# A transformer layer in split fp32: where the remainder of the down projection's weights is computed

## The chip, the cores and the metric

The kernel runs on one NeuronCore of one Trainium2 chip. The metric is device time in microseconds of one execution; lower is better. Before the change the median of 3 runs is 771.91 us (771.39 to 772.88).

## The reference

One layer of a diffusion backbone over 512 latent tokens and 128 context tokens, all in float32, with a model width of 1024 and an inner width of the feed-forward part of 2816. Each kind of token has its own modulation (scale, shift and gate made from a condition vector):

```python
mod = (jax.nn.silu(cond) @ w_ada + b_ada)[:, None, :]
sh1, sc1, g1, sh2, sc2, g2 = jnp.split(mod, 6, axis=-1)
h = _rms(x, norm_mix) * (1 + sc1) + sh1
mix, k, v = _mixer(h, rope, ctx_k, ctx_v, w_in, q_norm, k_norm, conv_w,
                   attn_out_norm, conv_out_norm, w_out)
x = x + g1 * mix
h2 = _rms(x, norm_ffn) * (1 + sc2) + sh2
gate, up = jnp.split(h2 @ w_gate_up, 2, axis=-1)
x = x + g2 * ((jax.nn.silu(gate) * up) @ w_down)
```

The mixer is grouped-query attention beside a short gated convolution. The change touches the last line alone: the product with `w_down`, a matrix of 2816 by 1024.

## The kernel before

All 640 tokens are worked on as five tiles of 128 (four latent, one context). The matrix products run on TensorE (PE) in fp32r, a rounded form of float32. To keep float32's accuracy each operand is split in a rounded part (hi) and the remainder (lo = operand − hi), and each product is made of three: hi·hi, lo·hi, hi·lo (`mm3`, lines 154 to 157). `split` (lines 150 to 152) makes the two parts: ScalarE (ACT) writes the rounded part (line 151), VectorE (DVE) subtracts it from the operand (line 152).

The weights arrive as a stream of blocks, planned in the order of their use. `load` (line 218) takes a buffer `wf` (three of them), issues the load from HBM on SP's queue (line 225), and calls `load_split` (line 237), which takes a buffer `wh` and a buffer `wl` (four of each) and splits the block into them. `W` (line 256) hands a block to its product and, before that, loads the blocks that come up to 3 places later (9 for gate and up blocks). The blocks of the first norm's output weights (`gain`) are scaled while they are split; all others take the plain path, line 244.

The feed-forward part works in four groups of 6, 6, 5 and 5 feature tiles of 128. In a group, gate and up products of each feature tile come first, in Winograd's form: seven products of 12 matmuls each, with operands that are quarters of the loaded blocks or sums of quarters (`op_load`, line 195). These operands are split too, into buffers of the same `wh` and `wl` rings, in turn. DVE makes the sums (line 207). Products leave PSUM by ACT's copies (`copy_of`, line 1125) and DVE's sums (lines 1138, 1154, 1157, 1164); the activations end as the split pair `gH`, `gL`.

Then the group's down projection runs (`down`): two halves of 512 output columns, and in each half blocks of two feature tiles (128 partitions by 2 × 512 values, 512 KB; in the groups of five the last block of a half holds one tile, 256 KB). There are 24 such blocks in all. The first block of a half is used up for all five token tiles; the second and third are used in turn, token tile by token tile. Each sum is multiplied by `g2` (line 1230) and added to `x2` (line 1231); in the last group the outputs are stored from there.

PE's instructions keep the order of the program. For the other engines a planner orders the instructions by priorities and its own estimate of their times; within an engine they then run in that order, and an instruction that waits holds up those behind it. `early(n)` moves instructions up by n places of priority; for the plain split n is `SOW` = −300, that is, back. A buffer of a ring is written again only when all readers of its last content are done.

POOL (GpSimd) makes some powers, sums and sums of quarters for the first four feature tiles (`SPO` = 4), and issues a few small loads near the start. DMA transfers are issued from SP's queue nearly always.

Of the kernel before, what the change touches and what calls it, by code (L numbers as in the profile page):

```python
# [15 lines left out]
P = 128  # L16
# [63 lines left out]
SOW = -300  # L80
# [11 lines left out]
def build(ctx, tc, x_prompt, x_sample, c, cache_k, cache_v, c_ctx, norm_mix, norm_ffn, w_ada, b_ada,  # L92
# [66 lines left out]
    def rstd_of(ss, n, scale, extra=None, tag="rs"):  # L159
        """(ss * scale + eps) ** -0.5 (times extra)"""  # L160
        w = ss.shape[1]
        ms = T("ms", (P, w), F32, 4)
        dve.tensor_scalar(ms, ss, scale, EPS, ALU.mult, ALU.add)
        r = T(tag, (P, w), F32, 6)
        pool.tensor_tensor(r, ms, neghalf[:, :w], ALU.pow)
        if extra is not None:
            dve.tensor_scalar_mul(r, r, extra)
        return r
# [7 lines left out]

# [1 line left out]
    x_dram = [x_sample[0, t * P:(t + 1) * P, :] for t in range(NL)] + [x_prompt[0]]  # L178
# [6 lines left out]

# [1 line left out]
    order, place, stream_at, phase = [], {}, [0], [0]  # L187
# [7 lines left out]
    def op_load(e):  # L195
        """one stationary operand of a gate and up block: a quarter of the block, or a sum of quarters"""
        f, name = e[0][1:]
        g, u = (order[place[x, f]][5] for x in "gu")
        a11, a12, a21, a22 = g[:, 0:4], g[:, 4:8], u[:, 0:4], u[:, 4:8]
        if name[0] == "S":  # L200
            if name == "S1":
                sums[f] = T("sx", (P, 2, 4, P), F32, 2)
            s13, s24 = sums[f][:, 0], sums[f][:, 1]
            src, x, y, op = {"S1": (s13, a21, a22, ALU.add), "S2": (s24, s13, a11, ALU.subtract),
                             "S3": (s13, a11, a21, ALU.subtract), "S4": (s24, a12, s24, ALU.subtract)}[name]
            with early(SOP[f >= NPLAIN]):
                (pool if f < SPO else dve).tensor_tensor(src, x, y, op)
        else:
            src = {"A11": a11, "A12": a12, "A21": a21, "A22": a22}[name]
        w = T(("wh", "wl")[ops[0] % 2], (P, 2, 4, P), F32R, WHB)  # L210
        ops[0] += 1
        with early(SOP[f >= NPLAIN]):
            split(w[:, 0], w[:, 1], src)
        e[5] = w
# [22 lines left out]
    def load_split(e, wf):  # L237
        key, src, ph, ring, gain, _ = e
        a, b = src.shape[1], src.shape[2]
        wh = T(ring + "h", (P, a, b), F32R, WHB)  # L240
        wl = T(ring + "l", (P, a, b), F32R, WHB)
        if gain is None:
            with early(SOQ[key[1]] if key[0] == 'q' else SOW):
                split(wh, wl, wf)
        else:
            for i in range(a):
                g = vec[:, gain + i:gain + i + 1]
                act.activation(wh[:, i], wf[:, i], AF.Copy, scale=g)
                dve.scalar_tensor_tensor(wl[:, i], wf[:, i], g, f32(wh[:, i]), ALU.mult, ALU.subtract)
        e[5] = (wh, wl)  # L250
# [61 lines left out]

# [1 line left out]
    crow = T("crow", (16, P))  # L314
# [3 lines left out]
    def ada1_load(k):  # L318
        """w_ada of feature tile k of the first norm's scale and shift"""
        out = []  # L320
        for h in range(2):
            wf = T("af", (P, 4, 2, P), F32, AFB)
            for i, col in enumerate((D + k * P, k * P)):
                sp.dma_start(wf[:, :, i], wa[:, 4 * h:4 * h + 4, col:col + P])
            out.append(wf)
            yield
        ada1[k] = out
        yield
# [41 lines left out]
    dve.tensor_copy(cs, cps.rearrange("p (c k) -> p k c", c=2))  # L370
    # products with the two conditions: four contraction tiles at a time on the four column groups of the
    # array, each with its conditions in the first columns; the groups' sums are added by sel afterwards
    dve.tensor_copy(cp[:, :, 0:2], cs)
# [11 lines left out]
    def vec_do():  # L385
        vps = PB((P, 64))
        pe.transpose(vps, rows, ident[:64, :64])
        dve.tensor_copy(vec[:, 0:64], vps)
        # (1 + b_sc) * norm for both norms
        for i, (bo, no) in enumerate(((8, V_MIX), (32, V_FFN))):  # L390
            dve.scalar_tensor_tensor(nb[:, i], vec[:, bo:bo + KD], 1.0, vec[:, no:no + KD], ALU.add, ALU.mult)

# [1 line left out]
    modA = [T(f"modA{i}", (P, KD, 2)) for i in range(2)]  # L394
    modB = [T(f"modB{i}", (P, KD, 2)) for i in range(2)]

    def mod_evict(i, f0, n, ps_sc, ps_sh):
        """ps_*: [P, n, 2] sums without bias for features f0..f0+n tiles"""
        no = (V_MIX, V_FFN)[i]
        bo = (0, 24)[i]  # L400
        if ps_sc is not None:
            tmp = T("modt", (P, n, 2), F32, 2)
            dve.tensor_tensor(tmp, ps_sc, vec[:, no + f0:no + f0 + n].unsqueeze(2).to_broadcast([P, n, 2]), ALU.mult)
            dve.tensor_tensor(modA[i][:, f0:f0 + n, :], tmp,
                              nb[:, i, f0:f0 + n].unsqueeze(2).to_broadcast([P, n, 2]), ALU.add)
        if ps_sh is not None:
            dve.tensor_tensor(modB[i][:, f0:f0 + n, :], ps_sh,
                              vec[:, bo + f0:bo + f0 + n].unsqueeze(2).to_broadcast([P, n, 2]), ALU.add)

# [1 line left out]
    hH = [T(f"hH{k}", (P, TOK), F32R) for k in range(KD)]  # L411
# [22 lines left out]
    def xT_do(t):  # L434
        """the normed tokens of tile t, feature-major"""
        both = PS2() if t < XB else None
# [121 lines left out]

# [1 line left out]
    rt = T("pr", (P, 2, NL, HD), F32, PRB)  # L560
# [19 lines left out]
    def head_norm(ps, nh, t, which):  # L580
        """rms over each head, gain, rotary; ps [P, nh*64] -> SBUF f32 [P, nh, 64]"""
        w = nh * HD
# [23 lines left out]

# [1 line left out]
    KA = T("KA", (P, NKV, 768), F32R)  # L608
# [52 lines left out]

# [1 line left out]
    g1 = [T("g1", (P, D), F32, 2) for _ in range(2)]  # L663
# [3 lines left out]
    CH = [(0, 320), (320, 320)]  # L667
    # (chunk, columns of the chunk, token columns, columns of the padded row)
    PIECES = [(0, slice(0, 320), slice(0, 320), slice(1, 321)),
# [106 lines left out]

# [1 line left out]
    of = [None] * NT  # L778
# [66 lines left out]
    def att_add(t, v, e):  # L845
        # the rows of the v lo products go to the other half of the partitions
        esw = T("es", (P, 2, P))
# [11 lines left out]

    # the context tokens' queries: four heads at a time  # L860
    cu = {}
# [45 lines left out]

# [1 line left out]
    units = [unit(t, v, p) for t in range(NL) for v in range(NKV) for p in range(2)]  # L909
# [35 lines left out]

# [1 line left out]
    if DSI:  # L947
# [32 lines left out]
    def g2_step(j, kp):  # L980
        """a quarter of g2's columns: sums over the contraction on the vector engine, then over partitions"""
        w = W(("ada", 5, j, kp))
# [18 lines left out]

    # second operands of the gate and up products: quarters of h2 (contraction half, token half) and their sums
    B = {}
# [79 lines left out]

    # ---- SwiGLU: a gate block and its up block by half the contraction against half the tokens, seven products
    # for the eight (Winograd's form) ----
    close_pool("psum")
# [15 lines left out]
    def plain(f, bs, toks):  # L1102
        """gate and up blocks of one half of the tokens by plain products"""
        ps = [FB(), FB()]
        for x, a in zip(ps, ("A1", "A2")):
            for i in (1, 2):
                prod(x, f, f"{a}{i}", bs[i - 1], i == 1, i == 2)
        if toks is LO:
            st[f] = T("cg", (P, TOK), F32, 2), T("cu", (P, TOK), F32, 2)
        cg, cu = st[f]  # L1110
        act.activation(cg[:, toks], ps[0][:, :HALF], AF.Silu)
        dve.tensor_tensor(cu[:, toks], ps[1][:, :HALF], cg[:, toks], ALU.mult)
        if toks is HI:
            ff_out(f, cu)
            del st[f]
# [161 lines left out]
def _rope_constants():  # L1277
    """cos and signed sin of the axial angles, [512 tokens, 64]: they depend on the shapes alone"""
    import numpy as np
# [36 lines left out]
```

## Time and profile before

| | before |
|---|---|
| runs, median (lowest to highest) | 771.91 us (771.39 to 772.88) |
| profiled execution, span from first to last instruction | 771.6 us |
| mean granted TensorE clock | 0.989 |
| bytes moved by DMA | 84.53 MB, mean 110 GB/s |
| down blocks loaded | 20 of 512 KB, 4 of 256 KB |
| down projection, four groups: PE from | 414.4, 532.4, 636.0, 732.6 us |
| last matmul ends | 767.7 us |

For the profiled execution the span is the only time that is given; it lies 0.3 us under the median of the runs. Busy times are per engine; PE is TensorE's matmuls, PEld its weight loads, which overlap them. A row of a timeline gives start, duration, engine, line, operation, the tile written and the tiles read; what stands in square brackets is idle time ahead of it and what ended that.

### The profile page before, as it was taken

Reading aid. Unit: us, or ns where it says so; the run is one execution under the profiler, and the core shown is the slowest. Engines: PE = TensorE matmul, PEld = TensorE weight load, DVE = VectorE, ACT = ScalarE, POOL = GpSimd, SP = SyncE. Lnnn points to the kernel's source line nnn. Section 1 sums busy time; section 2 is a strip of 40 time slices with the busy share of each in tenths; the row PEclk is TensorE's granted clock in tenths of the full one; section 3 lists DMA queues with packets and bytes.
Section 4 is the critical chain, followed back from the end, with each engine's and each line's share of the span. In section 5 each row is a group of like instructions: output and inputs, shape, how many; then the busy total and the mean of one; then the engine's idle time right before and its main releaser. Section 6 shows DMA issues by size and latency. Waiting matters only on the chain.

```text
span 771.6 us, 11961 instructions
## 1 busy us (share of the span) xinstructions
PE 744.2 (96%) x4580; PEld 669.2 (87%) x4580; DVE 563.1 (73%) x1033; ACT 376.8 (49%) x732; POOL 70.8 (9%) x97
## 2 busy tenths in 40 slices
PE   4999999999999999996999999999999999999997
PEld 3778988989999787886998789999889998899986
DVE  5566887675666799789778777984677866788653
ACT  5446676666665346875452125554125542255510
POOL 3105101011010330044100000000000000000000
PEclk9999999999999999999899999999999999999999
DMA  9984134424325433111134412233112231222312
GB/s 290 308 236 128 42 109 140 121 90 140 120 89 171 161 133 110 56 55 55 56 110 153 134 55 83 83 109 110 54 56 82 83 109 56 80 84 84 110 55 82
DMA packets 102350, 84.53 MB, mean 110 GB/s; under 512 B 4526, under 2 KB 82674, under 8 KB 102292
## 3 DMA queue, kind: packets, MB, share of 16 engines
q1 hardware_dynamic: 100980, 83.39, 35.0%
q8 instruction: 36, 0.59, 0.3%
q10 hardware_dynamic: 1056, 0.26, 0.2%
q0 software_dynamic: 256, 0.11, 0.1%
q14 instruction: 22, 0.18, 0.1%
HBM read 79.68 MB, written 2.75 MB: 107 GB/s over the span
## 4 chain that ended last, share of the span: by engine, by line
PE 83%; DVE 8%; ACT 3%; DMA 2%; issue 2%; SPq 2%; POOL 1%; ACTq 0%; POOLq 0%
PE pf L155 17%; PE pf L157 17%; PE pf L156 17%; PE pc L678 3%; PE pc L679 3%; PE pc L680 3%; PE ps L155 3%; PE ps L156 3%; PE ps L157 3%; PE po L833 2%; PE ps L790 2%; PE pt L816 2%; PE pc L380 2%; DMA af<-in_w_ada_dram 2%; DVE wl L152 1%
## 5 line engine op out<-in xcount | busy, mean ns | idle before, releaser
L151 ACT ACTIVATE wh<-wf 128x1024 fp32r<-128x1024 f32 (+1 forms) x76 | 64.1, 843 | 93.1 <-PE pf L157 63.2
L155 PE MATMUL pf<-wh,gH 128*128 128x512 f32 (+1 forms) x225 | 88.2, 392 | 0.0
L157 PE MATMUL pf<-wh,gL 128*128 128x512 f32 (+1 forms) x225 | 87.7, 390 | 0.0
L156 PE MATMUL pf<-wl,gH 128*128 128x512 f32 (+1 forms) x225 | 87.7, 390 | 0.0
L152 DVE TENSOR_TENSOR wl<-wf,wh 128x1024 fp32r<-128x1024 f32 (+1 forms) x42 | 49.4, 1176 | 27.8 <-ACT wh L151 24.9
L678 PE MATMUL pc<-hH,wh 128*128 128x320 f32 x192 | 61.7, 321 | 0.0
L679 PE MATMUL pc<-hL,wh 128*128 128x320 f32 x192 | 60.0, 312 | 0.0
L680 PE MATMUL pc<-hH,wl 128*128 128x320 f32 x192 | 59.9, 312 | 0.0
L155 PE MATMUL pf<-T,wh 128*128 128x320 f32 x160 | 50.1, 313 | 6.2 <-ACT p L1125 6.2
L155 PEld LDWEIGHTS pf<-wh,gH 128*128 128x128 f32 x225 | 42.3, 188 | 9.8 <-ACT wh L151 0.2
L157 PEld LDWEIGHTS pf<-wh,gL 128*128 128x128 f32 x225 | 42.3, 188 | 9.8
L156 PEld LDWEIGHTS pf<-wl,gH 128*128 128x128 f32 x225 | 42.3, 188 | 9.8 <-issue 0.2
L156 PE MATMUL pf<-T,wh 128*128 128x320 f32 x160 | 49.9, 312 | 0.0
L157 PE MATMUL pf<-T,wh 128*128 128x320 f32 x160 | 49.9, 312 | 0.0
L155 PE MATMUL pf<-T,wl 128*128 128x320 f32 x160 | 49.3, 308 | 0.0
L156 PE MATMUL pf<-T,wl 128*128 128x320 f32 x160 | 49.3, 308 | 0.0
L157 PE MATMUL pf<-T,wl 128*128 128x320 f32 x160 | 49.3, 308 | 0.0
L156 PE MATMUL pf<-B,wl 128*128 128x320 f32 x152 | 47.5, 313 | 0.3 <-DVE B L1020 0.3
L155 PE MATMUL pf<-B,wl 128*128 128x320 f32 x152 | 47.4, 312 | 0.0
L157 PE MATMUL pf<-B,wl 128*128 128x320 f32 x152 | 47.2, 310 | 0.0
L1230 DVE TENSOR_TENSOR dm<-pf,g 128x512 f32<-128x512 f32 (+1 forms) x41 | 27.7, 676 | 22.9 <-PE pf L157 22.9
L151 ACT ACTIVATE wl<-wf 128x512 fp32r<-128x512 f32 x34 | 21.4, 630 | 43.5 <-PE pf L156 36.8
(308 smaller groups left out, 2097.5 us busy)
## 6 DMA issues: line engine op xcount, KB each, us to landing
wf<-in_w_gate_up_dram SPq DMA_DIRECT2D x44, 512.0 KB, 3.8
aw<-in_w_ada_dram SPq DMA_DIRECT2D x24, 512.0 KB, 4.7
wf<-in_w_down_dram SPq DMA_DIRECT2D x20, 512.0 KB, 3.2
wf<-in_w_in_dram SPq DMA_DIRECT2D x18, 512.0 KB, 5.9
af<-in_w_ada_dram SPq DMA_DIRECT2D x32, 256.0 KB, 6.1
x<-in_x_sample_dram SPq DMA_DIRECT2D x8, 512.0 KB, 5.3
wf<-in_w_out_dram SPq DMA_DIRECT2D x8, 512.0 KB, 4.5
wf<-in_w_ada_dram SPq DMA_DIRECT2D x8, 512.0 KB, 3.8
```

What stands on the lines that cost most here:

```text
L151: act.activation(hi, src, AF.Copy)
L152: dve.tensor_tensor(lo, src, f32(hi), ALU.subtract)
L155: pe.matmul(out, lh, rh, start=start, stop=False, skip_group_check=more)
L156: pe.matmul(out, lh, rl, start=False, stop=False, skip_group_check=more)
L157: pe.matmul(out, ll, rh, start=False, stop=stop, skip_group_check=more)
L380: pe.matmul(out[CG * g:CG * (g + 1)], cp[:, k], w, start=(k < 4), stop=(k >= KD - 4), skip_group_check=True)
L678: pe.matmul(acc, wh[:, k], hH[k][:, c0:c0 + n], start=(k == 0), stop=False)
L679: pe.matmul(acc, wh[:, k], hL[k][:, c0:c0 + n], start=False, stop=False)
L680: pe.matmul(acc, wl[:, k], hH[k][:, c0:c0 + n], start=False, stop=(k == KD - 1))
L790: pe.matmul(s2[:, g, :320], q, kk[:, v, P + g * 320:P + (g + 1) * 320], start=(i == 0), stop=(i == 1))
L816: pe.transpose(tp[:, i, h], u[3][h][:, kt * P:(kt + 1) * P], ident)
L1230: dve.tensor_tensor(dm, ps[:, :n], g2[cc][:, oc], ALU.mult)
```

## The change

For a block of `w_down`, `split` is no longer called. ACT writes the rounded part into `wh` as before, and then, in a second pass over `wf`, the same with a scale of −1 into `wl`: the negated rounded part. POOL then issues a transfer that reads the same block once more from HBM and adds it onto `wl`. What stands in `wl` after it is block − rounded part, as before. All three carry the same low priority as the split had. The comments and descriptions that the diff also takes out are left out here.

```diff
         wh = T(ring + "h", (P, a, b), F32R, WHB)
         wl = T(ring + "l", (P, a, b), F32R, WHB)
-        if gain is None:
+        if key[0] == "d":
+
+            with early(SOW):
+                act.activation(wh, wf, AF.Copy)
+                act.activation(wl, wf, AF.Copy, scale=-1.0)
+                pool.dma_start(wl, src, accum_op=ALU.add)
+        elif gain is None:
             with early(SOQ[key[1]] if key[0] == 'q' else SOW):
                 split(wh, wl, wf)
         else:
```

## The prediction

> **What bounds the kernel now.** I read the page first, for the engines' shares, then the busy time by stages from the first down block on, then what the weight loads of TensorE (PEld) waited for, and last the timelines of ACT, DVE and PE around the 24 down blocks.
>
> ```profile
> PE 744.2 (96%) x4580; PEld 669.2 (87%) x4580; DVE 563.1 (73%) x1033; ACT 376.8 (49%) x732; POOL 70.8 (9%) x97
> ```
>
> ```profile
> core 0: us, PE busy (x) PEld busy (x) DVE busy (x) ACT busy (x) POOL busy (x), PEclk, DMA share, GB/s
> 402.00:768.00 366.00, 365.65 (x2109) 334.91 (x2108) 265.13 (x422) 137.09 (x240) 0.00 (x0) 1.00 0.28 87
> 414.00:437.00 23.00, 23.00 (x100) 18.07 (x98) 19.99 (x30) 5.54 (x7) 0.00 (x0) 1.00 0.51 160
> 460.00:530.00 70.00, 70.00 (x479) 70.00 (x478) 56.43 (x94) 38.63 (x71) 0.00 (x0) 1.00 0.31 96
> ```
>
> ```profile
> PEld pf L155 <- ACT p L1125: 6.4, 1, 6.4
> PEld pf L155 <- DVE cu L1154: 0.3, 1, 0.3
> ```
>
> The reader is to see three things. PE is busy for 365.65 of the 366 us in which every down block is rounded and used, at a granted clock of 1.00. DVE is busy for 265 of them and nothing on PE waits for it: the only wait of note after 366 us, 6.4 us, is for an ACT copy in a stage before the first down block is touched. And POOL does nothing at all in that time. So an instruction taken off DVE here can give at most 366.00 − 365.65 = 0.35 us. The change can only keep the time or cost something.
>
> **What is removed.** The 24 subtractions on DVE:
>
> ```profile
> L152 DVE TENSOR_TENSOR wl<-wf,wh x24: 685/1222/1226, 404.2 to 750.3; 128x1024 fp32r<-128x1024 f32 x20, 128x512 fp32r<-128x512 f32 x4
> ```
>
> 20 × 1.22 + 4 × 0.69 = 27.2 us of DVE, all under a busy PE: worth 0 to 0.35 us; I take 0.
>
> **What is added.** On ACT a second pass over each block (the negated rounded part), of the form of the one that is there:
>
> ```profile
> 552.24 1.06 ACT L151 ACTIVATE wh<-wf 128x1024 fp32r<-128x1024 f32 x1 [11.54 <-PE pf L157]
> 749.64 0.63 ACT L151 ACTIVATE wh<-wf 128x512 fp32r<-128x512 f32 x1 [8.74 <-PE pf L157]
> ```
>
> 20 × 1.06 + 4 × 0.63 = 23.7 us of ACT, which now is busy for 137 of the 366 us. Then one transfer from POOL's queue for each block. No row shows an accumulating transfer, so I bound it from its neighbours: plain loads of the same blocks from SP, and POOL's few small loads.
>
> ```profile
> wf<-in_w_down_dram SPq DMA_DIRECT2D x20, 512.0 KB, 3.2
> wf<-in_w_down_dram SPq DMA_DIRECT2D x4, 256.0 KB, 2.6
> gnq<-in_q_norm_dram POOLq DMA_DIRECT2D x1, 32.0 KB, 5.8
> gnk<-in_k_norm_dram POOLq DMA_DIRECT2D x1, 32.0 KB, 5.0
> ```
>
> ```profile
> 18.50 0.96 POOL L508 DMA_DIRECT2D gnq<-in_q_norm_dram  x1
> 19.45 0.56 POOL L508 DMA_DIRECT2D gnk<-in_k_norm_dram  x1
> 369.24 1.27 POOL L207 TENSOR_TENSOR sx<-wf,sx 128x512 f32<-128x512 f32 x1
> ```
>
> From SP, 256 KB more cost 3.2 − 2.6 = 0.6 us, so 512 KB move in about 1.2 us and 2.0 are fixed. An accumulating transfer also reads its destination: 1.2 more. POOL's issue takes 0.56 to 0.96. Lower bound 3.2 (as the plain load), upper bound 5.8 (POOL's slowest small landing, when the loads at the start crowd the queues) + 1.2 + 1.2 = 8.2. I take 3.2 + 1.2 + 0.96 = 5.4 us from issue to landing, an estimate, because the transfers of this stage meet a DMA share of 0.28, like the SP rows, while POOL's small rows come from the crowded start. The last work of POOL is the row at 369.24, so the 24 issues have nothing queued behind them, and SP's queue is not moved past anything. The transfers read 20 × 512 + 4 × 256 KB = 11 MB more, in 366 us about 30 GB/s on top of 87.
>
> The Trainium skill, DMA: Bandwidth & Descriptors, section "Anatomy of one DMA", gives a transfer issued from GpSimd about 2.0 us plus its bytes over 436 GB/s; for 512 KB that would be an estimate of 3.2 us, the same as the SP row here, and less than the POOL rows of 5.0 and 5.8 us show for 32 KB. By it the transfer would be hidden with more to spare; the page gives no time for an accumulating one.
>
> **Whether it is hidden.** wl of a block comes later than now, by the difference of (ACT pass + transfer) and (subtraction): 1.06 + 5.4 − 1.22 = 5.2 us. What hides it is the time between the rounding of a block and its first use, which PE fills with earlier products. The tightest two that I found:
>
> ```profile
> 553.33 1.23 DVE L152 TENSOR_TENSOR wl<-wf,wh 128x1024 fp32r<-128x1024 f32 x1 [1.12 <-ACT wh L151]
> 561.79 0.40 PE L155 MATMUL pf<-wh,gH 128*128 128x512 f32 x1
> 562.02 0.39 PE L156 MATMUL pf<-wl,gH 128*128 128x512 f32 x1
> ```
>
> ```profile
> 626.38 1.05 ACT L151 ACTIVATE wh<-wf 128x1024 fp32r<-128x1024 f32 x1
> 627.47 1.23 DVE L152 TENSOR_TENSOR wl<-wf,wh 128x1024 fp32r<-128x1024 f32 x1 [0.45 <-ACT wh L151]
> 636.22 0.40 PE L156 MATMUL pf<-wl,gH 128*128 128x512 f32 x1
> ```
>
> The first is the third block of a half (its buffer comes free at 552.24, when the second block of the half before is used up), the second the first block of a group. With both ACT passes back to back, 2.12 us, the transfer may take 562.02 − 552.24 − 2.12 = 7.7 us in the one and 636.22 − 626.38 − 2.12 = 7.7 us in the other. 5.4 fits with 2.3 to spare; 8.2 would miss by 0.5. The first block of all has more:
>
> ```profile
> 402.37 1.06 ACT L151 ACTIVATE wh<-wf 128x1024 fp32r<-128x1024 f32 x1 [1.12 <-PE pf L157]
> 405.89 1.06 ACT L151 ACTIVATE wh<-wf 128x1024 fp32r<-128x1024 f32 x1 [0.69 <-ACT gH L151]
> 407.66 1.23 DVE L152 TENSOR_TENSOR wl<-wf,wh 128x1024 fp32r<-128x1024 f32 x1 [1.47 <-ACT wh L151]
> 414.68 0.40 PE L156 MATMUL pf<-wl,gH 128*128 128x512 f32 x1
> ```
>
> 414.68 − 402.37 − 2.12 = 10.2 us, less a wait for the wl buffer. That wait is the new one on ACT: the subtraction at 407.66 began 0.7 us after its wh was done (405.89 + 1.06 = 406.95), so its buffer was freed by PE then, and 1.77 us after the wh buffer. ACT will stand there in order in DVE's place, up to 1.77 − 1.06 = 0.7 us, and behind it stand ACT's copies of product sums, for which DVE's sums and then PE wait:
>
> ```profile
> 411.18 0.44 ACT L1125 ACTIVATE u<-pf 128x320 f32<-128x320 f32 x1 [0.82 <-PE pf L157]
> 411.74 0.48 DVE L1154 TENSOR_TENSOR cu<-pf,u 128x320 f32<-128x320 f32 x1
> 412.69 0.31 PE L155 MATMUL pf<-B,wl 128*128 128x320 f32 x1
> ```
>
> This chain ends at 411.74 + 0.48 = 412.22 and PE needs it at 412.69: 0.47 us of slack. An ACT pass of 1.06 us just ahead of such a copy would cost PE 1.06 − 0.47 = 0.6 us. SOW = −300 sets the passes behind the copies in the planner's eyes, and ACT is busy for only 38.63 of the 70 us in that stage, so I take one such hit, 0.6 us, lower bound 0. The load buffer wf is now released after the second ACT pass in place of the subtraction: 2.12 against 1.06 + 1.22 us after the start of the rounding, no worse; if it came 1 us later, the next load from SP would, and only DVE's sums of quarters wait for those.
>
> **The sum.** Against the profiled execution, whose span is 771.6 us: −0 (DVE) + 0 (transfer hidden) + 0.6 (one copy delayed) = 772.2 us. The runs shown have a median of 771.91, 0.3 above that span and no more than their own spread; I leave the forecast at 772.2, no change that a measurement of this kernel can tell (about 0.2%, 1.5 us).
>
> **The rivals.**
> Late remainder (slower): the accumulating transfer takes more than 7.7 us from issue to landing, and PE stands at the first use of wl. The mechanism has one place, the weight load of line 156 in the down projection, and decides from 7.7 us on. For it: POOL's only rows are 5.0 and 5.8 us for a sixteenth of the bytes, and the read of the destination may be slower than a plain move. Against: the crowd at the start. Price: at 10 us the two tight blocks cost 2.3 each, and the others, whose slack runs from 9 us (four or so, as the first block after its buffer wait), about 0.6 each: 4.6 + 2.4 = 7.0, giving 779. At 12 us, 2 × 4.3 + 4 × 2.5 = 18.6, giving 790.
> The Trainium skill, SBUF — State Buffer, section "Who interferes with whom", speaks against the change: GpSimd, which writes the descriptors of such a transfer, shares ports with VectorE and stands still while a two-port VectorE instruction holds them, though tensor_tensor, nearly all of what DVE does here, is inferred not to block it. If every busy us of DVE blocked POOL (265 of 366), the issue would stretch from 0.96 to 0.96 / 0.28 = 3.4 us and the transfer to 7.9: an estimate just over the edge. No run here shows it yet.
> ACT in the way (slower): about half of the 24 passes fall into gate and up stages, and half of those are placed ahead of a copy: 6 × 0.6 = 3.6, plus waits of 0.7 for a buffer in two: 5.0, giving 776.6. For it: the slack of 0.47. Against: ACT's idle time and the priority.
> A gain (faster): the other instructions are placed anew around the shorter DVE queue and the 6.4 us wait at 366 us shrinks, say by half: 768.4. For it: nothing but that the planner sees a changed program. Against: the wait lies before the first down block.
> That the change does not do what it says would be a transfer that lands in no more time than the subtraction took: then all is as in the forecast.
>
> **How the numbers follow.** Hidden, 0.46 (772.2; its own range 771.0 to 773.4, all within 0.2% of 771.9); late remainder 0.35; ACT in the way 0.15; gain 0.04. Hence slower 0.50, same 0.46, faster 0.04. The range runs from 770.9, the whole of the 0.35 us and the runs' spread below the median, up to 784, where the late remainder is cut at about 11 us of transfer; the gain and the upper third of the late case, together 0.15, are left out.
>
> **What would show it.** Right: 24 rows of POOL issues of 0.6 to 1 us, landing in 4 to 7 us; ACT about 24 us busier, DVE 27 less; PE still without a gap from 402 to 768 us. Wrong: PEld waits at line 156 for a DMA of w_down into wl (late remainder), or PE waits at line 155 for ACT copies at line 1125's place in the new file or DVE sums behind them (ACT in the way).

## The result, and the profile after

The changed kernel takes 779.52 us (median of 4 runs, 776.72 to 782.83) against 771.67 before: a ratio of 1.0098, 95% interval 1.0073 to 1.0123. It is slower by about 1%. Its profiled execution is the fastest of the four, 776.72 us, with a span of 775.0; all later runs show the same 1.7 to 2.3 us around the span.

The page of the changed kernel, the lines that answer to those of before and to the prediction's terms (busy us and share; a queue's packets, MB and share; a group's busy us and mean ns, then idle time and its releaser; KB and median us to landing):

```profile
PE 744.1 (96%) x4580; PEld 667.3 (86%) x4580; DVE 538.2 (69%) x1009; ACT 397.5 (51%) x756; POOL 99.3 (13%) x121
...
q0 software_dynamic: 6272, 11.65, 8.6%
...
L247 POOL DMA_DIRECT2D wl<-in_w_down_dram x24 | 27.8, 1158 | 357.5 <-ACT wl L246 348.3
...
L246 ACT ACTIVATE wl<-wf 128x1024 fp32r<-128x1024 f32 (+1 forms) x24 | 23.6, 984 | 47.9 <-PE pf L156 44.2
...
wf<-in_w_down_dram SPq DMA_DIRECT2D x20, 512.0 KB, 3.6
wl<-in_w_down_dram POOLq DMA_DIRECT2D x20, 512.0 KB, 8.3
```

The 24 issues are there (27.8 us of POOL), ACT has its second pass (23.6 us), DVE is 563.1 − 538.2 = 24.9 us less busy. None of that moves PE's busy time. The number that stands out is 8.3 us to landing, where a plain load of the same block from SP has 3.6. What PE waited for, in the same kernel from 366 us on:

```profile
PE pf L156 <- DMA wl<-in_w_down_dram: 4.2, 1, 4.2
```

One wait, once, in the whole down projection. The timeline around it, rows of SP, ACT, POOL and PE in order of time:

```profile
405.66 0.37 SPq L225 DMA_DIRECT2D wf<-in_w_down_dram  x1
...
405.94 1.22 POOL L247 DMA_DIRECT2D wl<-in_w_down_dram  x1 [1.61 <-PE pf L157]
...
412.61 1.06 ACT L245 ACTIVATE wh<-wf 128x1024 fp32r<-128x1024 f32 x1 [4.41 <-DMA wf<-in_w_down_dram]
413.58 1.04 ACT L246 ACTIVATE wl<-wf 128x1024 fp32r<-128x1024 f32 x1
...
414.92 1.22 POOL L247 DMA_DIRECT2D wl<-in_w_down_dram  x1 [7.76 <-ACT wl L246]
...
419.43 0.40 PE L155 MATMUL pf<-wh,gH 128*128 128x512 f32 x1
424.08 0.79 PE L156 MATMUL pf<-wl,gH 128*128 128x512 f32 x1 [4.25 <-DMA wl<-in_w_down_dram]
```

The same load in the kernel before, its issue on SP and the ACT pass that waited for it:

```profile
408.91 0.37 SPq L225 DMA_DIRECT2D wf<-in_w_down_dram  x1
...
412.24 1.06 ACT L151 ACTIVATE wh<-wf 128x1024 fp32r<-128x1024 f32 x1 [0.62 <-DMA wf<-in_w_down_dram]
```

This is the third block of the first half of the first group. Two delays add up. Its plain load, issued on SP at 405.66, now ends the wait of ACT at 412.61: 6.9 us, where before it took 412.24 − 408.91 = 3.3. Beside it run the accumulating transfers of the two blocks ahead, issued at 403.04 and 405.94, which take 7.2 and 10.3 us to landing. Then its own transfer, issued at 414.92, releases PE at 424.08, 9.2 us later. Stages of the changed kernel around the stall (start and end, length, busy us and count of PE, PEld, DVE, ACT, POOL, granted clock, DMA share, GB/s):

```profile
411.00:419.80 8.80, 8.80 (x39) 6.76 (x37) 4.61 (x8) 3.11 (x4) 1.22 (x1) 1.00 0.87 186
419.80:424.10 4.30, 0.05 (x2) 0.03 (x1) 1.75 (x3) 0.00 (x0) 0.00 (x0) 0.76 0.90 277
424.10:428.00 3.90, 3.90 (x9) 3.11 (x10) 3.65 (x6) 2.00 (x2) 0.18 (x1) 0.50 0.34 105
428.00:432.00 4.00, 4.00 (x17) 3.16 (x16) 2.52 (x4) 2.01 (x2) 1.53 (x2) 0.90 0.78 224
...
436.00:440.00 4.00, 4.00 (x17) 2.73 (x16) 0.00 (x0) 2.52 (x3) 1.20 (x1) 1.00 1.12 231
```

The DMA engines are nearly full here: 0.87 and 0.90 of their time, later 1.12 (in this view the share can pass 1), and 0.85 from 411 to 440 us as a whole; before, the first down stage had 0.51. And the stall costs more than its length: when PE starts again, its granted clock is 0.50, and only later 1.00. From the first matmul of the first half to that of the second are 440.02 − 411.03 = 29.0 us, against 436.76 − 414.44 = 22.3 before: 6.7 us lost, of them 4.25 of standing still and 2.4 at the lower clock. The half speed lasts from 422.0 to 428.8; finer stretches show its two ends (0.67 over half a microsecond is one third of it at full speed):

```profile
421.50:422.00 0.50, 0.00 (x0) 0.00 (x0) 0.05 (x1) 0.00 (x0) 0.00 (x0) 1.00 1.04 324
422.00:422.50 0.50, 0.00 (x0) 0.00 (x0) 0.00 (x0) 0.00 (x0) 0.00 (x0) 0.50 1.01 332
...
428.50:429.00 0.50, 0.50 (x3) 0.43 (x2) 0.50 (x1) 0.00 (x0) 0.50 (x1) 0.67 0.36 41
429.00:429.50 0.50, 0.50 (x4) 0.41 (x3) 0.17 (x1) 0.32 (x1) 0.02 (x1) 1.00 0.71 164
```

PE works at half speed from 424.08 to 428.8, 4.7 us, and half of that is the 2.4. The other groups lost nothing that counts: from first to last matmul their down projections take 42.0, 35.0 and 35.2 us, against 42.0, 35.0 and 35.1 before.

### The profile page after: what moved, and what is told of

Same layout as the page of the kernel before. It is cut to its first block, busy times and chain, and to the rows that moved or that the text cites. A ratio compares the mean times of both kernels' runs of the same rounds, so it can differ in the third digit from the quotient of the medians.

```text
span 775.0 us, 12020 instructions
## 1 busy us (share of the span) xinstructions
PE 744.1 (96%) x4580; PEld 667.3 (86%) x4580; DVE 538.2 (69%) x1009; ACT 397.5 (51%) x756; POOL 99.3 (13%) x121
## 3 DMA queue, kind: packets, MB, share of 16 engines
q0 software_dynamic: 6272, 11.65, 8.6%
## 4 chain that ended last, share of the span: by engine, by line
PE 80%; DVE 8%; DMA 3%; ACT 3%; issue 3%; SPq 1%; POOL 1%; DVEq 0%; POOLq 0%; ACTq 0%
PE pf L156 17%; PE pf L155 17%; PE pf L157 17%; PE pc L684 3%; PE pc L685 3%; PE pc L686 3%; PE ps L155 3%; PE ps L156 3%; PE ps L157 3%; PE po L839 2%; PE ps L796 2%; PE pt L822 2%; PE pc L386 2%; DMA af<-in_w_ada_dram 2%; DMA wl<-in_w_down_dram 1%
## 5 line engine op out<-in xcount | busy, mean ns | idle before, releaser
L247 POOL DMA_DIRECT2D wl<-in_w_down_dram x24 | 27.8, 1158 | 357.5 <-ACT wl L246 348.3
L151 ACT ACTIVATE wh<-wf 128x512 fp32r<-128x512 f32 (+1 forms) x52 | 40.4, 777 | 25.5 <-DMA wf<-in_w_in_dram 8.1
L246 ACT ACTIVATE wl<-wf 128x1024 fp32r<-128x1024 f32 (+1 forms) x24 | 23.6, 984 | 47.9 <-PE pf L156 44.2
```

The source lines that it names most:

```text
L151: act.activation(hi, src, AF.Copy)
L246: act.activation(wl, wf, AF.Copy, scale=-1.0)
L247: pool.dma_start(wl, src, accum_op=ALU.add)
```

## The experiments

Each was timed beside runs of the kernel before on the same chip; every ratio is against those, with its 95% interval.

**The kernel before once more.** No edit.

> The kernel before, unchanged, to see how far its own trace moves from run to run. In the trace of the change, all of TensorE's work up to the first down block began 3.4 us earlier than before (411.0 against 414.4 us), although the order of the instructions on every engine is the same up to there. Theory A (that lead is chance): this trace also begins its down projection 1 to 3 us off 414.4. Theory B (the change brings the lead): this trace is within 0.5 us of 414.4. It also shows how much time lies around the span: 0 to 0.3 us if the first profile is typical, 1.7 if the change adds nothing there.

One execution, 770.6 us, span 768.8. Its first down matmul:

```profile
411.60 0.40 PE L155 MATMUL pf<-wh,gH 128*128 128x512 f32 x1
```

That is 2.8 us earlier than in the first trace of the same kernel, so the 3.4 us lead of the changed kernel's trace ahead of the down projection is chance (theory A). The time lies 1.8 us above the span, so the execution whose span of 771.6 the prediction used was a somewhat long one, and its 0.3 us below the median of the runs is not the time around the span. In the twelve traces of all kernels here the first down matmul starts anywhere from 411.0 to 415.4 us. Differences of spans between single traces therefore mean nothing below some 4 us; the stage from 411 to 440 us, taken by itself, does.

**The change once more.** No edit.

> The changed kernel, unchanged, because its four runs spread over 6 us (776.7 to 782.8) and the profiled one was the fastest. Theory late remainder: the time above 776.7 is more stalls of the same kind, TensorE waiting at line 156 for the accumulating transfer of other blocks, or a longer one in the first group, with a half-speed clock for some 4 us after each. Rival: the clock is throttled in the slower runs without a stall.

1.0065 (1.0047 to 1.0083), 777.16 us. The profiled execution, 778.95 us, has one wait again, at the same place and longer:

```profile
PE pf L156 <- DMA wl<-in_w_down_dram: 5.8, 1, 5.8
```

The stage from half to half takes 29.8 us here. The load on SP took 8.8 us this time, the transfer 8.8. For this trace the rival falls: from 380 to 760 us the clock is low only around the stall. But the longer stall explains little of the spread. This span is 2.2 us longer than that of the first trace of the change; the stage makes 0.8 of it, and 1.5 lie ahead of the first down matmul (412.49 against 411.03), where traces differ by chance. What the slowest runs, up to 782.8, lost beyond that was not traced.

**The ACT pass without the transfer.**

```diff
-                pool.dma_start(wl, src, accum_op=ALU.add)
+                dve.tensor_tensor(wl, wf, f32(wl), ALU.add)
```

> The second ACT pass stays, but VectorE adds the block onto the negated rounded part instead of the transfer from POOL. Theory late remainder (the transfer is the cost): the time of before, 771 to 773 us, no wait of TensorE from the first down block on. Rival ACT in the way (the pass is the cost): 775 or more, with TensorE waiting for ACT's copies or for VectorE's sums behind them.

0.9998 (0.9988 to 1.0008). From the first down block on PE waits for nothing; its one wait after 366 us, 5.1 us for an ACT copy, is the one that the kernel before has there too (6.2). ACT in the way is refuted: the second pass costs nothing that can be measured, and the loss hangs on the transfer.

**The transfer without the addition.**

```diff
-                pool.dma_start(wl, src, accum_op=ALU.add)
+                pool.dma_start(wl, src)
```

> Leaves out the addition: POOL's transfer overwrites wl with the block, so the output is not the reference's; all waits and bytes read from HBM are the same. If it is the accumulation that takes long (reading the destination), landings fall from a median of 8.3 us to 4 to 5 and the stall of 4.2 us in the first group shrinks to 1 us or less: 772 to 775 us. If it is POOL's queue itself, landings stay at 7 to 8 us and the time at 776 to 780.

1.0006 (0.9993 to 1.0019), no stall in the down projection. Landings, the share of POOL's queue, and one issue, in this kernel:

```profile
wl<-in_w_down_dram POOLq DMA_DIRECT2D x20, 512.0 KB, 4.9
...
q0 software_dynamic: 6272, 11.65, 5.2%
```

```profile
415.89 0.72 POOL L247 DMA_DIRECT2D wl<-in_w_down_dram  x1 [5.25 <-DVE cg L1170]
```

The same queue, the same bytes from HBM, the same waits: 4.9 us instead of 8.3, 0.72 us of issue instead of 1.2, and 5.2% of the DMA engines' time instead of 8.6% for the same 11.65 MB. So it is the accumulation that takes long, both in what POOL does for an issue and in the transfer. POOL's queue has the smaller part: the plain loads from SP take 3.7 us in this run.

**Only the third block of the first half of group one.**

```diff
-        if key[0] == "d":
+        if key == ("d", 4, 0):
```

> Only one of the 24 blocks goes the new way: the third of the first half of the first group, at which TensorE stood in both traces of the change (4.2 and 5.8 us). The other 23 are subtracted on VectorE as before. Theory two delays (this block's plain load on SP's queue is slowed from 3.3 to 7 to 9 us by the accumulating transfers of the two blocks ahead, and then its own transfer takes 9): here the load takes 3.3 to 4 us again, and the transfer alone 6 to 8; the stall is 0 to 1 us, time 771 to 773. Rival (the accumulating transfer alone is too long for this block's slack): it takes 9 us again, a stall of 1 to 3 us and a slow clock after it, 774 to 776.

1.0004 (0.9991 to 1.0016), no stall. The load on SP and what it released, in this kernel; then the one accumulating transfer:

```profile
407.61 0.37 SPq L225 DMA_DIRECT2D wf<-in_w_down_dram  x1
...
411.01 1.06 ACT L245 ACTIVATE wh<-wf 128x1024 fp32r<-128x1024 f32 x1 [0.69 <-DMA wf<-in_w_down_dram]
```

```profile
wl<-in_w_down_dram POOLq DMA_DIRECT2D x1, 512.0 KB, 7.2
```

The load is back at 3.4 us, the transfer takes 7.2, and it fits: issued at 413.33, landed 420.5, first needed at 421.77. Its own length alone is not too long for this block, though 1.2 us is all that is left.

**All but the first two blocks**, so that nothing accumulates beside the load of the third.

```diff
-        if key[0] == "d":
+        if key[0] == "d" and key not in (("d", 0, 0), ("d", 2, 0)):
```

> 22 blocks go the new way, the first two of the first half of the first group are subtracted on VectorE, so that no accumulating transfer runs beside the plain load of the third. Theory two delays: that load takes 3.3 to 5 us, the third block's own transfer 7 to 9, and the stall falls from 4.2 to 5.8 us to 0 to 2: 771 to 774 us. Rival (own length alone): the stall stays at 4 us or more.

1.0004 (0.9986 to 1.0021), no stall in the profiled execution. The load took 3.4 us, the third block's transfer 7.0. With 22 of 24 transfers in place the loss is gone: the two transfers beside that load made the stall at the third block. They lengthened both parts, its load (6.9 us with them, 3.4 without) and its own transfer (9.1 and 7.0). Which of the two weighs more was not tried. One of its ten runs still took 776.6 us; it was not traced, so what it waited for stays open.

**All but the third block.**

```diff
-        if key[0] == "d":
+        if key[0] == "d" and key != ("d", 4, 0):
```

> The reverse: 23 blocks go the new way, the third block of the first half of the first group is subtracted on VectorE. Theory two delays: no stall of TensorE anywhere, since all the others had slack in both traces, 771 to 773 us; the plain load of the third block still takes 7 to 9 us. Rival (the loss is spread over the groups, the traces showed only one part of it): 775 or more.

1.0055 (1.0029 to 1.0082), runs from 770.1 to 780.6. The expected 771 to 773 is wrong, though not in the way of the rival: the wait moved on by one block.

```profile
PE pf L155 <- DVE dm L1236: 2.7, 1, 2.7
PE pf L156 <- DMA wl<-in_w_down_dram: 0.7, 1, 0.7
```

PE now stands 0.7 us for the transfer of the first block of the second half, and then 2.7 us for VectorE, at a PSUM bank that it has not emptied. VectorE stood at a sum of quarters of the next group, whose load came late; the row here, then the one of the change:

```profile
443.88 0.69 DVE L207 TENSOR_TENSOR sx<-wf 128x512 f32<-128x512 f32 x1 [12.72 <-DMA wf<-in_w_gate_up_dram]
...
442.16 0.69 DVE L207 TENSOR_TENSOR sx<-wf 128x512 f32<-128x512 f32 x1 [7.44 <-DMA wf<-in_w_gate_up_dram]
```

In the change PE comes to the second half 29.0 us after the first down matmul, here after 22.3; there its own stall, and the low clock behind it, left VectorE the time, and PE did not feel the 7.44 us.

**The third block used last.** In the first half of group one the second block is used up ahead of the third.

```diff
-            for fs in blocks[:-2]:
+            lead = blocks[:-1] if gi == 0 and j == 0 else blocks[:-2]
+            for fs in lead:
...
-                    for fs in blocks[-2:]:
+                    for fs in blocks[len(lead):]:
```

> All 24 blocks go the new way, but in the first half of the first group the second block is used up for all token tiles ahead of the third, so that the third is first needed 5.6 us later (24 matmuls of 0.233 us). Theory late remainder: the transfer is as long as before, the stall goes to 0 to 0.5 us, and the time to 771 to 773. Rival (the transfers cost TensorE something besides that wait): the stall goes and the time stays at 775 or more.

1.0143 (1.0124 to 1.0162): the stall at the third block goes, and the kernel is slower than the change. Neither expectation held as it stood. PE's waits (the 1.6 us are at the first block of the second half), and the rows of VectorE that explain the longer one:

```profile
PE pf L155 <- DVE dm L1237: 5.3, 1, 5.3
PE pf L156 <- DMA wl<-in_w_down_dram: 1.6, 1, 1.6
```

```profile
430.02 0.68 DVE L1237 TENSOR_TENSOR dm<-pf,g 128x512 f32<-128x512 f32 x1
444.51 0.69 DVE L207 TENSOR_TENSOR sx<-wf 128x512 f32<-128x512 f32 x1 [13.81 <-DMA wf<-in_w_gate_up_dram]
445.12 0.69 DVE L1238 TENSOR_TENSOR x<-dm,x 128x512 f32<-128x512 f32 x1
```

VectorE's queue stands 13.81 us at a sum of quarters of the next group, whose plain load takes 12.5 us beside the transfers (5.0 in the kernel before, 10.9 in the change); behind it, in order, are the products and sums that empty PSUM. So a second price of the crowd is that loads which VectorE needs come late, and PE then has no bank to write to. In this version all five sums of the first half are finished in its last 7 us, so more of them are left behind that instruction: it had passed two of them before it stood still, against three in the change.

**Groups two to four only, and group one only.**

```diff
-        if key[0] == "d":
+        if key[0] == "d" and key[1] >= 6:
```

> The 18 blocks of groups two to four go the new way, the six of the first group are subtracted on VectorE. Theory crowd in the first group (only there do the loads of w_ada for g2 run beside the down blocks, and the DMA share lies near 0.9): no wait of TensorE, 771 to 773 us, the ratio within 0.2% of 1. Rival (transfers of 8 to 10 us cost something in every group): 773.5 or more.

1.0001 (0.9987 to 1.0016), no wait of PE. With `< 6` in place of `>= 6`:

> The reverse: only the six blocks of the first group go the new way. Theory crowd in the first group: the whole loss of the change, 776 to 779 us, with the stall at the third block. Rival as above: no more than half of the loss, under 775.

1.0093 (1.0069 to 1.0117), with a stall of 5.6 us at the third block:

```profile
PE pf L156 <- DMA wl<-in_w_down_dram: 5.6, 1, 5.6
```

The median of 780.4 lies a little above what was expected. Six of the 24 blocks carry the whole loss; the other 18 cost nothing, though their transfers take nearly as long (a median of 7.9 us with groups two to four alone, 9.0 with group one alone). The traces show a difference in slack: in the change the transfer of group two's third block takes 9.3 us too, but is issued 1.6 us ahead of the group's first down matmul and lands 0.9 us ahead of its use; in group one it is issued 3.9 us after that matmul. With groups two to four alone, the gate and up loads issued in group one's down stage land in 5.0 us again. No version here beats the kernel before: the best ones equal it.

## Why the prediction went as it did

The forecast itself, a hidden transfer and 772.2 us, was wrong by 7.3 us. That 779.5 lies inside the stated range is due to the rival, late remainder, for which the range had been drawn out to 784.

**What could be gained.** Right: PE's gap of 0.35 us was all there was. With the 24 subtractions gone and no stall (the transfer without the addition) the ratio is 1.0006.

**ACT.** The pass was priced right (23.7 us predicted, 23.6 measured). The one hit of 0.6 us that the sum took for it does not show: with the pass alone PE waits nowhere for it, and the ratio is 0.9998.

**The transfer: the step that failed.** The sum took 5.4 us from issue to landing, "because the transfers of this stage meet a DMA share of 0.28". Measured: a median of 8.3, and 9.1 at the block that stalled. Two of its terms were too small. The addition was priced at 1.2 us; the run without it shows 8.3 − 4.9 = 3.4 in the median, and for the second last block, beside which no load runs, 6.0 − 4.1 = 1.9. An issue took POOL 1.16 us in the mean, not 0.96. And the share of 0.28 is that of a kernel without these transfers. Around the second group's first down blocks, before and after:

```profile
521.00:545.00 24.00, 23.98 (x132) 21.24 (x132) 12.15 (x16) 8.21 (x13) 0.00 (x0) 1.00 0.33 110
...
524.00:548.00 24.00, 24.00 (x134) 21.55 (x133) 6.48 (x11) 13.10 (x18) 6.02 (x5) 1.00 0.87 192
```

In groups three and four it is 0.26 and 0.20 before, 0.71 and 0.74 after. So most of the share that a transfer meets comes from the transfers themselves; in group one the loads of w_ada add to it (0.51 before, 0.85 after). With little beside them the transfers come near the estimate. Two answers for the changed kernel, all transfers from w_down (plain ones included), then the stretch from 743 to 760 us alone, where no load runs beside them, only the stores of the outputs (minimum, median, maximum):

```profile
DMA to landing us min/median/max: 2.7/7.2/10.5
...
DMA to landing us min/median/max: 3.7/4.8/6.0
```

In the second, 6.0 us are 512 KB and 3.7 are 256 KB. The shortest of 512 KB, 5.5 us, was issued at 628.25, and a load ran beside only its second half. The 10.5 of the first answer is an accumulating transfer of the last group's first half, above the upper bound of 8.2, which had left the transfers' effect on each other out. The estimate by the Trainium skill (DMA: Bandwidth & Descriptors, "Anatomy of one DMA"), 2.0 us plus the bytes over 436 GB/s, is 3.2 us for 512 KB; every accumulating transfer of 512 KB seen here took longer, 5.5 us at least.

**The side effect on SP's queue.** The prediction held that "SP's queue is not moved past anything" and left the plain loads at their old times. In the queue that is so; in the DMA engines it is not. The load of the third block went from 3.3 to 6.9 and 8.8 us, which is 3.6 us where the stall of the profiled run was 4.25.

**Whether it is hidden.** The two tightest blocks that were named, with 7.7 us, did not stall. For the first block of its group the planner issued the transfer at 628.25, 10.9 us ahead of its use; the third block of the half at 556 landed 0.6 us ahead of it. The block that did stall had more on paper. Its first use in the kernel before:

```profile
423.08 0.39 PE L156 MATMUL pf<-wl,gH 128*128 128x512 f32 x1
```

423.08 − 412.24 − 2.12 = 8.7 us. Its late load took 3.6 of that, which left 5.1 for a transfer of 9.2. The prediction had taken the slack block by block, but with the loads where they lay before.

**The rivals.** Late remainder came true in its place, line 156. That its 779 (at a transfer of 10 us) meets the measured time is luck: it summed small stalls over six blocks, of which the two that it named did not stall, and there is one long one, at a block that it did not name, whose load was late too, with the low clock behind it, 2.4 us that no term had. ACT in the way: refuted. That DVE blocks POOL's issues, by the Trainium skill's rule (SBUF — State Buffer, "Who interferes with whom"): the issue took 1.20 us from 436 to 440 us, with DVE idle throughout, and no more than 1.29 anywhere, where the rival had 3.4; nothing of it shows.

## What to carry to other kernels

A stage that is hidden behind a full engine is hidden only as long as its slack; take the slack block by block, and take the DMA share of the very stretch, with the new transfers in it. A transfer put beside loads that others wait for is to be charged with their delay too. When one stall is taken away by giving its block more time, look for what that stall had been covering: here it covered the next block and the emptying of PSUM.

## What the runs showed of the hardware

An accumulating transfer of 512 KB from HBM into SBUF took 5.5 to 10.5 us in the change, 6.0 with only output stores beside it; a plain one from the same queue took 4.9 in the median, and its issue 0.72 us of POOL against 1.2. Whether it is the reading of the destination or the adding that takes the time was not tried. A load from SP of 512 KB, 3.3 us in the kernel before, took 6.9 and 8.8 beside two such transfers; one of w_gate_up, 5.0 before, took up to 12.5.

The granted clock fell to 0.50 at 422.0, 2.2 us after PE's last matmul, and stood there until 428.8, 6.8 us, at a stall of 4.25. The change once more has 6.8 us too (423.3 to 430.1) at a stall of 5.8, and group one only (427.6 to 434.4) at one of 5.6. At the stall of 2.7 us in all but the third block it is 3.4 us (445.6 to 449.0), all of it after PE had gone on at 445.2. So what a stall costs beyond its length is half of that part of the low time that falls on work: 2.4 us here, 1.5 in the change once more (427.1 to 430.1), although its stall was longer. The Trainium skill (TensorE: Matmul & The Clock Gate, "Part 1: The HAM clock gate") says that an idle window of about 3.4 us halves the clock and a busy one of that length restores it. The low times measured, 3.4 and twice that, agree with its length; the moments, 2.2 us after PE stopped and 4.7 after it went on, are not 3.4 us from the stall's ends.
